# Down-projection in float32r: each product of 128 rows as two of 64 rows, with two accumulators

## The chip, the core and the metric

The kernel runs on one core of a Trainium2 chip. The time is the device time of one execution in microseconds; before the change it is 773.02 us in the median of three runs (772.6 to 773.74). A smaller time is better. A profiled execution gives the trace that this document reads. In it PE is TensorE's matmuls, PEld its weight loads, DVE is VectorE, ACT is ScalarE, POOL is GpSimd, SP is SyncE, whose queue issues most transfers.

## The reference

One layer of a causal decoder on 512 tokens of width 1024: an HGRN2 mixer and an S5 mixer side by side, a gated merge with an output projection, a conv-gated MLP, and a gated input embedding (PLE) with a last RMSNorm. The change lies in the last product of the MLP:

```python
def _conv_gated_ffn(h, w_up, conv_w, conv_b, w_down):
    a = h @ w_up                                   # (512, 1024) @ (1024, 5632)
    ...
    gate, val = jnp.split(c, 2, axis=-1)
    return (jax.nn.gelu(gate) * val) @ w_down      # (512, 2816) @ (2816, 1024)

x = x + _conv_gated_ffn(_rmsnorm(x, norm_ffn_g[i]), w_up[i], conv_w[i], conv_b[i], w_down[i])
ple_gate = jax.nn.sigmoid(_rmsnorm(x, norm_ple_g[i]) @ w_ple_gate[i])
x = x + ple_gate * (p[i] @ w_ple_proj[i])
return _rmsnorm(x, norm_final_g)
```

Everything is float32.

## The kernel before

Activations lie with their features on the 128 partitions and the 512 tokens along the free dimension. Every large product takes its operands in two float32r parts, a high one (a copy rounded to float32r) and a low one (what the rounding left), and adds three matmuls into one PSUM bank: high weights by high activations, high by low, low by high. `mm3` (L229) issues these three, at L231, L232 and L233, and then calls `tick`, which advances side work by an estimated clock.

Weights stream from HBM in pieces of at most 1024 columns (`emit_w`, L202 issues the transfer into `wst`, of which there are two). `split` (L243 on ScalarE, L244 on VectorE) makes `whi` and `wlo`, of which three pairs exist. For the last stage, the gates, the pairs are called `wgh` and `wgl` and all eight stay in place.

The MLP's up-projection (`pup`, `pug`, `puv`) leaves 22 row blocks of 128 features as pairs `gh`, `gl`. The down-projection runs four passes (`mp2`). In each, two blocks of 128 output features are summed over the 22 row blocks, one bank each (`pdn`): 22 x 2 x 3 = 132 products a pass, 528 in all. After a pass `finish_x` adds each sum to the residual `xr` (L945, VectorE), makes the split pair `x2gh` (L946, ScalarE) and `x2gl` (L947, VectorE), and squares `xr` (L953, ScalarE); GpSimd adds the squares up in `sqs` (L954). During the following pass a side generator transposes the two finished blocks on TensorE, four transposes a block (`ptk`, L1031), and ScalarE copies them out (L1033).

After the last pass come the PLE projection (`ppe`), with the transposes of the last two blocks between, the sums over `sqs` (`psq`), and the gates (`pga`, then `pgb`).

TensorE's order is the order in which the program is written. The other engines' orders are made by a scheduler, which puts `split` of weights at high priority; so instructions added on VectorE can move others. There are four large PSUM buffers (`main_ps`) and four for small uses (`small_ps`), a bank each; `pdn` takes large ones, `ptk` and `psq` small ones.

Of the kernel before, what the change touches and what calls it, by code (L numbers as in the profile page):

```python
# [12 lines left out]
ALU = mybir.AluOpType  # L13
# [3 lines left out]
P = 128  # L17
# [4 lines left out]
NJ = FF // P  # L22
# [91 lines left out]
def hybrid_kernel(ctx: ExitStack, tc: tile.TileContext, a):  # L114
    nc = tc.nc
    V, S, G, E = nc.vector, nc.scalar, nc.gpsimd, nc.tensor
# [13 lines left out]
    def main_ps(name):  # L130
        return psm.tile([P, 512], F32, tag="main", name=name)

    def small_ps(name):
        return pss.tile([P, 512], F32, tag="small", name=name)
# [8 lines left out]
    def small(name, j=0, w=1):  # L143
        return sm[:, OFF[name] + j: OFF[name] + j + w]
# [4 lines left out]
    clock = [0.0]  # L149
    sides = []  # L150

    def tick():
        for sd in list(sides):
            if sd[0] <= clock[0]:
                d = next(sd[1], None)
                if d is None:
                    sides.remove(sd)
                else:
                    sd[0] = clock[0] + d

    def side(gen, delay=0.0):
        sides.append([clock[0] + delay, gen])
        return sides[-1]
# [61 lines left out]
    def get_w():  # L225
        prefetch_w()
        return wstate["ready"].pop(0)

    def mm3(out, w, x, start, stop):  # L229
        (wh, wl), (xh, xl) = w, x  # L230
        E.matmul(out, wh, xh, start=start, stop=False)  # L231
        E.matmul(out, wh, xl, start=False, stop=False)  # L232
        E.matmul(out, wl, xh, start=False, stop=stop)  # L233
        clock[0] += 0.65
        tick()

    def cols(w, kk, width, c0, n=P):

        return tuple(t[:, kk * width + c0: kk * width + c0 + n] for t in w)
# [6 lines left out]
    def act_pair(name):  # L246
        return (ap_.tile([P, KD, T], F32R, tag="ahi", name=name + "h"),
                ap_.tile([P, KD, T], F32R, tag="alo", name=name + "l"))
# [140 lines left out]
    def k_outer(name, out4, x, then=None):  # L389

        ps = [main_ps(f"{name}{m}") for m in range(4)]
        k = 0
        while k < KD:
            nk = plan[wstate["next"] - len(wstate["ready"])][0][2]
            w = get_w()
            for kk in range(nk):
                for m in range(4):
                    mm3(ps[m], cols(w, kk, 512, m * P), rows(x, k), k == 0, k == KD - 1)
                k += 1
        if then:  # L400
            then()
        for m in range(4):
            out4(m, ps[m])
# [28 lines left out]
    def phase_v():  # L432
        ps = [main_ps(f"psv{t}") for t in range(4)]
        for k0 in range(0, KD, 2):
            w = get_w()
            for kk in range(2):
                k = k0 + kk
                for t in range(4):
                    mm3(ps[t], tuple(x[:, k, t * P:(t + 1) * P] for x in xg), cols(w, kk, 512, 0, 512),
                        k == 0, k == KD - 1)  # L440
        for t in range(4):
            S.activation(vt[t], ps[t], AF.Copy, scale=rr1[:, t:t + 1])
# [17 lines left out]
    def proj(name, pool=main_ps):  # L460
        w = get_w()
        ps = pool(name)
        for k in range(KD):
            mm3(ps, cols(w, k, P, 0), rows(xg, k), k == 0, k == KD - 1)
        return ps
# [453 lines left out]
    for m in range(KD):  # L919
        w = get_w()  # L920
        ps = [main_ps(f"pbh{m}"), main_ps(f"pbs{m}")]
# [3 lines left out]
        a_, b_ = (sig[m][:, i] for i in range(2))  # L925
# [9 lines left out]
    xr = xp.tile([P, KD, T], F32, name="xr")  # L935
# [6 lines left out]
    def finish_x(m, ps, x, g):  # L942

        xm = xr[:, m]
        V.tensor_tensor(out=xm, in0=xm, in1=ps, op=ALU.add)  # L945
        S.activation(x[0][:, m], xm, AF.Copy, scale=small(g, m))  # L946
        V.scalar_tensor_tensor(out=x[1][:, m], in0=xm, scalar=small(g, m), in1=x[0][:, m].bitcast(F32),  # L947
                               op0=ALU.mult, op1=ALU.subtract)
        if m == 0:
            S.activation(sqs, xm, AF.Square)  # L950
        else:
            sq = xp.tile([P, T], F32, tag="sq", bufs=2, name=f"sq{m}")
            S.activation(sq, xm, AF.Square)  # L953
            G.tensor_tensor(out=sqs, in0=sqs, in1=sq, op=ALU.add)  # L954
# [17 lines left out]
    for m in range(4, KD):  # L972
        w = get_w()
        ps = main_ps(f"pw{m}")
# [8 lines left out]
    gs_ = [(gpool.tile([P, T], F32R, name=f"gh{j}"), gpool.tile([P, T], F32R, name=f"gl{j}")) for j in range(NJ)]  # L983
# [19 lines left out]
    ps = [main_ps(f"pup{i}") for i in range(4)]  # L1003
    r2 = r2_sums()
    next(r2)
    for k0 in range(0, KD, 2):
        w = get_w()
# [7 lines left out]
    for j in range(2, NJ):  # L1015
        ps = [main_ps(f"pug{j}"), main_ps(f"puv{j}")]
        for k0 in (0, 4):
            w = get_w()
# [16 lines left out]
    def tok_side(ms):  # L1035
        for m in ms:
            to_tokens(m)
            yield 0.0

    x2 = act_pair("x2g")  # L1040
    for mp2 in range(KD // 2):
        ps = [main_ps(f"pdn{mp2}_{i}") for i in range(2)]
        for k0 in range(0, NJ, 4):
            w = get_w()
            for kk in range(min(4, NJ - k0)):
                k = k0 + kk
                for i in range(2):
                    mm3(ps[i], cols(w, kk, 256, i * P), gs_[k], k == 0, k == NJ - 1)
        for i in range(2):
            finish_x(mp2 * 2 + i, ps[i], x2, "g_ple")  # L1050
        if mp2 < 3:
            side(tok_side((mp2 * 2, mp2 * 2 + 1)), 8.0)

# [49 lines left out]
    ps = [[main_ps(f"pga{t}{c}") for c in range(2)] for t in range(2)]  # L1103
# [90 lines left out]
def build(arrays):  # L1194
    import concourse.bacc as bacc
    nc = bacc.Bacc("TRN2", target_bir_lowering=False, num_devices=1, dynamic_dma_scratch_size=8192)
    args = {n: nc.dram_tensor(n, v.shape, mybir.dt.from_np(v.dtype), kind="ExternalInput").ap()
            for n, v in arrays.items()}
    args["out"] = nc.dram_tensor("out", (4, P, D), F32, kind="ExternalOutput").ap()
    with tile.TileContext(nc) as tc:  # L1200
        hybrid_kernel(tc, args)
    return nc
# [9 lines left out]
```

## Time and profile before

| what | value |
| --- | --- |
| median of three runs | 773.02 us |
| the profiled execution | 772.75 us |
| its span, first to last instruction | 771.0 us |
| granted TensorE clock, mean over the span | 0.998 |
| PE busy | 759.0 us (98%) |
| DVE busy | 517.6 us (67%) |
| ACT busy | 367.5 us (48%) |
| POOL busy | 54.6 us (7%) |
| down-projection, first product to end of the last | 585.10 to 707.60 us |

A group of instructions reads: line, engine, operation, what is written and read (buffer numbers left out), shape, count, then busy time in us, mean ns of one, idle time before them. A matmul's shape `128*64 128x512` is rows times columns of the array, then what streams. A timeline row begins with start and duration in us. A row of a stretch gives its bounds and length, then for each engine that works there the busy time and the count, the granted clock, the DMA share and GB/s. Matmuls overlap, so a matmul's duration is not its price: the distance of starts is. After a change of what the engine does, a matmul's start is shown at the start of its load.

### The profile page before, as it was taken

To read this page: it belongs to the slowest core of one execution; us is meant where nothing else is said; L and a number is where in the kernel's file an instruction comes from. 1 tells how busy PE (TensorE), PEld (TensorE's weight loads), DVE (VectorE), ACT (ScalarE), POOL (GpSimd) and SP (SyncE) were. 2 spreads that over 40 slices of the span, in tenths; PEclk is the share of its full clock that TensorE was granted. 3 is DMA by queue.
4 is the path that set the end of the run, shared out by engine and by line. 5 is a ranking of instruction groups with operands and counts; after the bars stand their busy time and mean duration, and the time that the engine had idled before them with its cause. 6 is when DMAs were issued, how large, how long until landed. Compare 5 with 4: busy or idle time off the path is not lost.

```text
span 771.0 us, 10253 instructions
## 1 busy us (share of the span) xinstructions
PE 759.0 (98%) x3966; PEld 627.7 (81%) x3966; DVE 517.6 (67%) x851; ACT 367.5 (48%) x480; POOL 54.6 (7%) x96
## 2 busy tenths in 40 slices
PE   9999999999999999999999999999999999999996
PEld 7887888888887888888888888888888888888885
DVE  6999897798946675467976677677776324144555
ACT  7364583775748533342634344434434223234465
POOL 2030110010010000041000000000000001011000
PEclk9999999999999999999999999999999999999999
DMA  8573443243443323532232323232322332233511
GB/s 333 211 179 100 108 104 106 69 114 101 110 110 96 110 82 126 179 106 93 99 101 91 109 82 110 83 109 86 107 91 87 95 109 91 90 96 136 164 55 54
DMA packets 27039, 86.37 MB, mean 112 GB/s; under 512 B 4720, under 2 KB 4864, under 8 KB 26992
## 3 DMA queue, kind: packets, MB, share of 16 engines
q1 hardware_dynamic: 22608, 77.84, 30.7%
q0 software_dynamic: 3664, 6.84, 4.0%
q10 hardware_dynamic: 720, 1.05, 0.4%
q8 instruction: 31, 0.51, 0.3%
q14 instruction: 16, 0.13, 0.1%
HBM read 80.98 MB, written 4.69 MB: 111 GB/s over the span
## 4 chain that ended last, share of the span: by engine, by line
PE 90%; DVE 5%; DMA 2%; ACT 1%; issue 1%; POOL 0%; DVEq 0%; ACTq 0%
PE pdn L233 5%; PE pdn L231 5%; PE pdn L232 5%; PE puv L231 5%; PE puv L233 5%; PE pug L231 5%; PE pug L232 5%; PE pug L233 5%; PE puv L232 5%; PE pw L231 2%; PE pw L232 2%; PE pw L233 2%; PE pgs L231 2%; PE pgh L231 2%; PE pgs L233 2%; PE pgs L232 2%
## 5 line engine op out<-in xcount | busy, mean ns | idle before, releaser
L243 ACT ACTIVATE whi<-wst 128x1024 fp32r<-128x1024 f32 (+1 forms) x124 | 128.8, 1038 | 253.5 <-issue 75.1
L244 DVE TENSOR_TENSOR wlo<-wst,whi 128x1024 fp32r<-128x1024 f32 (+1 forms) x124 | 148.4, 1197 | 115.1 <-ACT whi L243 115.0
L231 PE MATMUL pdn<-gh,whi 128*128 128x512 f32 x176 | 69.1, 393 | 0.0
L233 PE MATMUL pdn<-gh,wlo 128*128 128x512 f32 x176 | 68.6, 390 | 0.0
L232 PE MATMUL pdn<-gl,whi 128*128 128x512 f32 x176 | 68.6, 390 | 0.0
L232 PE MATMUL pug<-x1gl,whi 128*128 128x512 f32 x160 | 62.3, 390 | 0.0
L233 PE MATMUL puv<-x1gh,wlo 128*128 128x512 f32 x160 | 62.3, 390 | 0.0
L231 PE MATMUL puv<-x1gh,whi 128*128 128x512 f32 x160 | 62.3, 390 | 0.0
L231 PE MATMUL pug<-x1gh,whi 128*128 128x512 f32 x160 | 62.3, 389 | 0.0
L232 PE MATMUL puv<-x1gl,whi 128*128 128x512 f32 x160 | 62.3, 389 | 0.0
L233 PE MATMUL pug<-x1gh,wlo 128*128 128x512 f32 x160 | 62.3, 389 | 0.0
L992 DVE TENSOR_TENSOR u<-pug,R 128x512 f32<-128x512 f32 x20 | 13.8, 692 | 38.4 <-PE pug L233 38.4
L954 POOL TENSOR_TENSOR sqs<-sqs,sq 128x512 f32<-128x512 f32 x14 | 23.2, 1658 | 229.1 <-ACT sq L953 225.0
L233 PEld LDWEIGHTS pdn<-gh,wlo 128*128 128x128 f32 x176 | 33.0, 188 | 6.9
L232 PEld LDWEIGHTS pdn<-gl,whi 128*128 128x128 f32 x176 | 33.1, 188 | 6.7
L231 PEld LDWEIGHTS pdn<-gh,whi 128*128 128x128 f32 x176 | 33.1, 188 | 6.6
L233 PEld LDWEIGHTS puv<-x1gh,wlo 128*128 128x128 f32 x160 | 30.1, 188 | 6.3
L232 PEld LDWEIGHTS pug<-x1gl,whi 128*128 128x128 f32 x160 | 30.1, 188 | 6.2
L233 PEld LDWEIGHTS pug<-x1gh,wlo 128*128 128x128 f32 x160 | 30.0, 188 | 6.3
L232 PEld LDWEIGHTS puv<-x1gl,whi 128*128 128x128 f32 x160 | 30.0, 188 | 6.2
L231 PEld LDWEIGHTS puv<-x1gh,whi 128*128 128x128 f32 x160 | 30.1, 188 | 6.1
L231 PEld LDWEIGHTS pug<-x1gh,whi 128*128 128x128 f32 x160 | 30.0, 188 | 6.2
(391 smaller groups left out, 1751.6 us busy)
## 6 DMA issues: line engine op xcount, KB each, us to landing
wst<-W SPq DMA_DIRECT2D x126, 512.0 KB, 3.3
xt<-x SPq DMA_DIRECT2D x4, 512.0 KB, 9.2
T<-d_k POOLq DMA_DIRECT2D x4, 512.0 KB, 8.6
xr<-xT SPq DMA_DIRECT2D x4, 512.0 KB, 6.4
wst<-W SPq DMA_DIRECT2D x6, 256.0 KB, 2.5
xs<-xT SPq DMA_DIRECT2D x4, 256.0 KB, 5.4
xs<-xT SPq DMA_DIRECT2D x2, 512.0 KB, 6.4
d_u<-uT POOLq DMA_DIRECT2D x4, 256.0 KB, 5.0
```

The lines of the kernel that those rows point to most:

```text
L231: E.matmul(out, wh, xh, start=start, stop=False)
L232: E.matmul(out, wh, xl, start=False, stop=False)
L233: E.matmul(out, wl, xh, start=False, stop=stop)
L243: S.activation(hi, src, AF.Copy)
L244: return V.tensor_tensor(out=lo, in0=src, in1=hi.bitcast(F32), op=ALU.subtract)
L954: G.tensor_tensor(out=sqs, in0=sqs, in1=sq, op=ALU.add)
L992: V.tensor_tensor(out=u[:, 2:], in0=ps[i], in1=Rt, op=ALU.mult)
```

## The change

Each product of the down-projection is issued as two, with the same moving columns and weight columns: one on partitions 0 to 63, one on partitions 64 to 127. The first adds into `pdn`, a large buffer, the second into a new accumulator `pdm`, a small one. After a pass VectorE adds `pdm` to the residual (a new instruction, L1061 of the changed program) before `finish_x` adds `pdn`. Ten lines come in ahead, so L231 is still `mm3`'s, and what was L244, L945, L947 and L1031 stands at L254, L955, L957 and L1041.

```diff
+    def mm3_rows(outs, w, x, start, stop):
+
+        (wh, wl), (xh, xl) = w, x
+        for i, (a_, b_) in enumerate(((wh, xh), (wh, xl), (wl, xh))):
+            for r, o in enumerate(outs):
+                rr = slice(r * 64, (r + 1) * 64)
+                E.matmul(o, a_[rr], b_[rr], start=start and i == 0, stop=stop and i == 2)
+        clock[0] += 0.65
+        tick()
...
     for mp2 in range(KD // 2):
-        ps = [main_ps(f"pdn{mp2}_{i}") for i in range(2)]
+        ps = [(main_ps(f"pdn{mp2}_{i}"), small_ps(f"pdm{mp2}_{i}")) for i in range(2)]
...
-                    mm3(ps[i], cols(w, kk, 256, i * P), gs_[k], k == 0, k == NJ - 1)
+                    mm3_rows(ps[i], cols(w, kk, 256, i * P), gs_[k], k == 0, k == NJ - 1)
         for i in range(2):
-            finish_x(mp2 * 2 + i, ps[i], x2, "g_ple")
+            m = mp2 * 2 + i
+            V.tensor_tensor(out=xr[:, m], in0=xr[:, m], in1=ps[i][1], op=ALU.add)
+            finish_x(m, ps[i][0], x2, "g_ple")
```

On TensorE, the first row block of the first pass before (the two output blocks are `pdn_0` and `pdn_1`):

```order
L231 MATMUL pdn_0_4989<-gh_3153,whi_4906 128x512
L232 MATMUL pdn_0_4989<-gl_3154,whi_4906 128x512
L233 MATMUL pdn_0_4989<-gh_3153,wlo_4907 128x512
L231 MATMUL pdn_1_4990<-gh_3153,whi_4906 128x512
L232 MATMUL pdn_1_4990<-gl_3154,whi_4906 128x512
L233 MATMUL pdn_1_4990<-gh_3153,wlo_4907 128x512
```

and in the changed program:

```order
L243 MATMUL pdn_0_4989<-gh_3153,whi_4906 128x512
L243 MATMUL pdm_0_4990<-gh_3153,whi_4906 128x512
L243 MATMUL pdn_0_4989<-gl_3154,whi_4906 128x512
L243 MATMUL pdm_0_4990<-gl_3154,whi_4906 128x512
L243 MATMUL pdn_0_4989<-gh_3153,wlo_4907 128x512
L243 MATMUL pdm_0_4990<-gh_3153,wlo_4907 128x512
L243 MATMUL pdn_1_4991<-gh_3153,whi_4906 128x512
L243 MATMUL pdm_1_4992<-gh_3153,whi_4906 128x512
```

The halves of a product follow each other, and every second instruction goes to the other half and bank: 1056 instead of 528. The transposes stand between the same products as before.

On VectorE, the end of the fourth pass before (`wlo` is the split of the last piece for `ppe`, `wgl` those of the first gate pieces):

```order
L945 TENSOR_TENSOR xr<-xr,pdn_0_5557 128x512
L945 TENSOR_TENSOR xr<-xr,pdn_1_5558 128x512
L244 TENSOR_TENSOR wlo_5754<-wst_5751,whi_5753 128x1024
L947 SCALAR_TENSOR_TENSOR x2gl<-xr,sm,x2gh 128x512 x2
L244 TENSOR_TENSOR wgl_5765<-wst_5780,wgh_5764 128x1024
```

and in the changed program:

```order
L1061 TENSOR_TENSOR xr<-xr,pdm_0_5966 128x512
L955 TENSOR_TENSOR xr<-xr,pdn_0_5965 128x512
L1061 TENSOR_TENSOR xr<-xr,pdm_1_5968 128x512
L254 TENSOR_TENSOR wlo_6298<-wst_6295,whi_6297 128x1024
L254 TENSOR_TENSOR wgl_6309<-wst_6324,wgh_6308 128x1024
L957 SCALAR_TENSOR_TENSOR x2gl<-xr,sm,x2gh 128x512
L955 TENSOR_TENSOR xr<-xr,pdn_1_5967 128x512
L957 SCALAR_TENSOR_TENSOR x2gl<-xr,sm,x2gh 128x512
```

The last addition to the residual has moved behind two weight splits and one `x2gl`. On ScalarE, after the same pass, the changed program has

```order
L253 ACTIVATE whi_6297<-wst_6295 128x1024
L253 ACTIVATE wgh_6308<-wst_6324 128x1024
L956 ACTIVATE x2gh<-xr,sm 128x512
L963 ACTIVATE sq_6285<-xr 128x512
L1085 ACTIVATE pe<-ppe_6356 128x512
L1085 ACTIVATE pe<-ppe_6364 128x512
L1085 ACTIVATE pe<-ppe_6372 128x512
L956 ACTIVATE x2gh<-xr,sm 128x512
L963 ACTIVATE sq_6292<-xr 128x512
```

where before both pairs of `x2gh` and square stood ahead of the gate's `wgh` and of the copies `pe`. The last square, which `psq` on TensorE waits for by way of GpSimd, is now last of these nine.

## The prediction

> **What bounds the kernel now.** First the page: busy time, then the chain of work that ended last, then the down-projection's group.
>
> ```profile
> span 771.0 us, 10253 instructions
> ...
> PE 759.0 (98%) x3966; PEld 627.7 (81%) x3966; DVE 517.6 (67%) x851; ACT 367.5 (48%) x480; POOL 54.6 (7%) x96
> ...
> PE 90%; DVE 5%; DMA 2%; ACT 1%; issue 1%; POOL 0%; DVEq 0%; ACTq 0%
> ...
> L231 PE MATMUL pdn<-gh,whi 128*128 128x512 f32 x176 | 69.1, 393 | 0.0
> ```
>
> TensorE carries the chain and never idles before these products. The third view is the busy time of the stretch from the first product of the down-projection to the end of the last: all work, then the tile `pdn` alone, then the transposes `ptk` alone.
>
> ```profile
> 585.10:707.60 122.50, 122.50 (x554) 101.50 (x553) 42.55 (x45) 36.74 (x47) 8.21 (x5) 1.00 0.29 91
> ...
> 585.10:707.60 122.50, 121.35 (x528) 98.51 (x527) 4.59 (x7) 1.00 0.29 91
> ...
> 585.10:707.60 122.50, 3.60 (x24) 2.99 (x24) 3.58 (x6) 1.00 0.29 91
> ```
>
> 528 products and 24 transposes fill 122.50 us without a gap (PE busy 122.50); VectorE is busy for a third of it (42.55), ScalarE for less. So the price of one product decides. Not its 393 ns, which overlap, but the distance between starts. The timeline, matmuls and then weight loads:
>
> ```profile
> 599.83 0.39 PE L233 MATMUL pdn<-gh,wlo 128*128 128x512 f32 x1
> ...
> 602.10 0.39 PE L231 MATMUL pdn<-gh,whi 128*128 128x512 f32 x1
> ...
> 599.83 0.19 PEld L231 LDWEIGHTS pdn<-gh,whi 128*128 128x128 f32 x1
> 600.06 0.19 PEld L232 LDWEIGHTS pdn<-gl,whi 128*128 128x128 f32 x1
> ```
>
> From 599.83 to 602.10 lie ten products: **0.227 us each**, and 528 x 0.227 = 119.9 us. Each load starts when the product before starts and is over (0.19) before that product has streamed: loading is hidden already. What the change is worth is therefore 528 times what a pair of halves costs above or below 0.227, and whatever surrounds the pairs.
>
> The Trainium skill, page "TensorE: Matmul & The Clock Gate", section "Part 3: Packing small matmuls", says that a weight load overlaps running matmuls only where the row groups differ; by that rule loads of full height lie open today and the split would hide them, a gain. The rows of 599.83 disagree: the load runs inside the product before it, on the same rows.
>
> **The pair of halves.** Every product becomes two, on rows 0 to 63 and 64 to 127, each with all 128 weight columns and all 512 moving columns. If halves run in turn, a pair costs 2 x 0.227 = 0.454. If they run side by side, it costs what one does, provided that two loads fit. How fast loads can follow one another, and what a shorter product costs:
>
> ```profile
> 125.27 0.64 PEld L172 LDWEIGHTS pu<-vt,b 128*128 128x128 f32 x5
> ...
> 762.52 0.28 PE L231 MATMUL ppe<-whi,whi 128*128 128x256 f32 x1
> ...
> 763.59 0.28 PE L231 MATMUL ppe<-whi,whi 128*128 128x256 f32 x1
> ```
>
> Five loads in 0.64, the last of them 0.19 long: (0.64 - 0.19) / 4 = 0.113 from load to load. Two loads one after the other take 0.226, just inside 0.227; overlapped, they take less. Nine products of 256 columns lie between 762.52 and 763.59: 0.119 each, so the second 256 columns of a full product cost 0.108 and 512 would cost 0.216 without the fixed part of 0.011. Lower bound of a pair: 0.216, if that fixed part vanished behind the other half (528 x 0.011 = 5.8 us gained). Upper bound: 0.454 (528 x 0.227 = 119.9 us lost).
>
> Which end? The trace holds no product on half the rows, but products on half and quarter columns of the array; the chain gives their pace, the groups their shapes.
>
> ```profile
> 125.42 0.67 PE pu L172 x6
> 126.09 1.08 PE ps5v L172 x32
> ...
> 153.47 0.57 PE ps5k L758 x16
> ...
> L172 PE MATMUL ps5v<-uy,et 128*64 128x64 f32 x128 | 4.6, 225 | 0.0
> ...
> L172 PE MATMUL pu<-vt,b 128*128 128x128 f32 x24 | 3.3, 274 | 0.0
> L758 PE MATMUL ps5k<-F,Bb 128*32 128x128 f32 x64 | 2.6, 279 | 0.0
> ```
>
> A full-array pass of 128 moving columns takes 0.67 / 6 = 0.112. The passes of `ps5k` move 128 columns too, on four column strips in turn: 0.57 / 16 = 0.036, a third. Half-width `ps5v` passes of 64 columns cost 0.034 where half of 0.112 is 0.056. Products on different parts of the array do run together here, their loads too. Row halves differ in one thing: column strips write different partitions of PSUM, row halves write the same 128 partitions of two banks at once. No row shows that; I take the value of the strips, **0.227 a pair, 0 us**, and keep both ends.
>
> The same section of the Trainium skill puts about 4 ns of issue time on each further tile of a pack. By it, an estimate, the stage would lose 528 x 0.004 = 2.1 us more; no row here shows row tiles.
>
> **Changing the mode.** Going between full-array and partial products costs. Into `ps5y` (half columns) and out of it, loads and matmul:
>
> ```profile
> 139.93 0.19 PEld L233 LDWEIGHTS pgs<-xgh,wlo 128*128 128x128 f32 x1
> 140.47 0.20 PEld L172 LDWEIGHTS ps5y<-st,F 128*64 128x64 f32 x4 [0.35 <-issue]
> ...
> 140.15 0.39 PE L233 MATMUL pgs<-xgh,wlo 128*128 128x512 f32 x1
> ...
> 142.21 0.20 PEld L172 LDWEIGHTS ps5y<-uy,T 128*64 128x64 f32 x4
> 142.48 0.19 PEld L231 LDWEIGHTS pgh<-xgh,whi 128*128 128x128 f32 x1
> 142.59 0.19 PEld L232 LDWEIGHTS pgh<-xgl,whi 128*128 128x128 f32 x1
> ```
>
> The last full product starts at 140.15 and has streamed at 140.38; the first load of the new mode waits until 140.47 instead of following at 140.16. So 0.09 of emptying, and the load is no longer hidden: 0.11 for 128 columns. 0.20 per change. On the way out the last of four loads starts near 142.27, its product is through near 142.38, and the next full product streams when the second load follows, 142.59: 0.21. In the down-projection the transposes are full-array:
>
> ```profile
> 623.63 0.59 PEld L1031 LDWEIGHTS ptk<-sm,xr 128*128 128x128 f32 x4
> 624.19 0.19 PEld L231 LDWEIGHTS pdn<-gh,whi 128*128 128x128 f32 x1
> 624.30 0.19 PEld L232 LDWEIGHTS pdn<-gl,whi 128*128 128x128 f32 x1
> ```
>
> Today their first load starts with the last product before them, at no cost. There are 24 / 4 = 6 groups, each with a change in and one out, and the stage's own entry and exit: 14 changes x 0.205 = **+2.9 us**. Nothing hides them, since TensorE is the chain.
>
> **The second sums and the order behind them.** Eight more additions on VectorE of about 0.69 (half of the 1.37 below): 5.5 us on an engine that is busy for a third of the stage; off the path. From the third pass on the new accumulators take the banks of the transposes of the pass before, which run some 8 us into a pass of 122.5 / 4 = 30.6 us; ScalarE has emptied them long before the next pass starts, and no product waits for a bank. At the end of the stage the order changes, and TensorE soon needs the sum of squares:
>
> ```profile
> 707.12 1.37 DVE L945 TENSOR_TENSOR xr<-xr,pdn 128x512 f32<-128x512 f32 x2
> ...
> 707.57 1.06 ACT L243 ACTIVATE whi<-wst 128x1024 fp32r<-128x1024 f32 x1 [1.66 <-PE pdn L232]
> ...
> 710.28 0.61 ACT L953 ACTIVATE sq<-xr 128x512 f32<-128x512 f32 x1
> 710.80 1.05 ACT L243 ACTIVATE wgh<-wst 128x1024 fp32r<-128x1024 f32 x1
> ...
> 709.90 3.50 POOL L954 TENSOR_TENSOR sqs<-sqs,sq 128x512 f32<-128x512 f32 x2 [27.39 <-ACT sq L953]
> ...
> 716.46 1.08 PEld L172 LDWEIGHTS psq<-ones,sqs 128*128 128x128 f32 x8
> ...
> L244 DVE TENSOR_TENSOR wgl<-wst,wgh 128x1024 fp32r<-128x1024 f32 x8 | 10.9, 1362 | 7.1 <-ACT wgh L243 7.1
> L947 DVE SCALAR_TENSOR_TENSOR x2gl<-xr,sm,x2gh 128x512 fp32r<-128x512 f32 x8 | 8.7, 1134 | 0.0
> ```
>
> `psq` is issued at 716.46; the sums were ready at 709.90 + 3.50 = 713.40, 3.1 us early. Now the last addition stands behind `wgh`, `wgl` and one `x2gl`. If the gate weights land by 710.80, the latest that this row allows: wgh to 711.85, wgl to 713.2, x2gl to 714.35, addition to 715.0, x2gh (0.7) and square (0.61) to 716.3, POOL (1.75) to 718.1: TensorE waits 1.4. If they land by 708.63, when `whi` ends: wgl follows the other split (from 709.2, 1.23) at 710.4 and all is some 1.5 earlier: no wait. I take **+0.7**. Queued behind `psq` are only gate products, which come later by as much.
>
> **Sum.** The profiled execution took 772.75 us, 0.27 below the median of 773.02: 772.75 + 0 + 2.9 + 0.7 = 776.35. I say **776.5 us**; this case alone holds 774.8 to 779 (four ns a pair, 0 to 1.4 at the end, the changes at half to one and a half).
>
> **Rivals.**
> *The halves run in turn*, because both write the same partitions, or because the program's half is run like a full product. For it: no row shows two writers of one partition. Against: strips share everything else and overlap. 772.75 + 119.9 + 3.6 = 896.
> *A load must be finished before the other half's may begin*: 2 x 0.188 = 0.376 a pair, + 78.7 + 3.6 = 855. Against it: loads follow at 0.113.
> *Some contention*, a few to 40 ns a pair (loads fit by only 0.001): 0.240 would give 772.75 + 6.9 + 3.6 = 783, 0.260 gives 794.
> *Faster*: one half's fixed 0.011 passes behind the other's stream, since two products now stand at the array. It decides once it saves over 3.6 / 528 = 0.007 a pair; all of it gives 772.75 - 5.8 + 3.6 = 770.6. Against it: each half keeps its own row of load, product, load; only what the two share could shrink, and the rows do not say that the 0.011 is shared.
>
> **How the numbers follow.** Forecast 0.60, in turn 0.11, serial loads 0.03, contention 0.12, faster 0.14. About 0.2% (1.5 us) is what a measurement can tell here. Faster than that: most of the last case, 0.10. Same: the rest of it and the low edge of the forecast, 0.13. Slower: 0.77. For 8 in 10 the range leaves out 896 and 855 (0.14), the worst contention (0.03) and the best gain (0.03): 770 to 792.
>
> **What would show it.** In the new profile the two halves' rows start a few ns apart and pairs 0.227 apart; `pdn` and `pdm` together have 1056 matmuls in about 125.4 us; before each `ptk` group and after it the loads pause by 0.2; `psq` starts up to 1.4 late. Pairs 0.45 apart, or halves of 0.227 in turn, would refute the core of it; pairs under 0.220 would make the change a gain.

## The result

| | median, us | lowest to highest |
| --- | --- | --- |
| the kernel before (9 executions) | 773.02 | 772.22 to 775.46 |
| the changed kernel (9 executions) | 778.16 | 775.55 to 779.42 |

The ratio is 1.0063, with a 95% interval of 1.0047 to 1.0078: slower by 0.6%. The profiled execution of the changed kernel took 778.16 us; the one of before took 772.75.

### The profile page after: what moved, and what is told of

Same layout as the page of the kernel before. It is cut to its first block, busy times and chain, and to the rows that moved or that the text cites. A ratio compares the mean times of both kernels' runs of the same rounds, so it can differ in the third digit from the quotient of the medians.

```text
span 776.4 us, 11316 instructions
## 1 busy us (share of the span) xinstructions
PE 762.3 (98%) x4494; PEld 626.8 (81%) x4494; DVE 521.7 (67%) x859; ACT 368.0 (47%) x480; POOL 53.0 (7%) x96
## 4 chain that ended last, share of the span: by engine, by line
PE 85%; DVE 6%; DMA 5%; ACT 2%; issue 1%; SPq 0%; POOL 0%; ACTq 0%; DVEq 0%
PE pdm L243 9%; PE pdn L243 6%; PE pug L233 5%; PE puv L233 5%; PE puv L231 5%; PE pug L231 5%; PE puv L232 5%; PE pug L232 5%; PE pw L233 2%; PE pw L232 2%; PE pw L231 2%; PE pgh L231 2%; PE pgs L231 2%; PE pgs L233 2%; PE pgs L232 2%; PE pgh L232 2%
## 5 line engine op out<-in xcount | busy, mean ns | idle before, releaser
L254 DVE TENSOR_TENSOR wlo<-wst,whi 128x1024 fp32r<-128x1024 f32 (+1 forms) x124 | 149.0, 1202 | 111.1 <-ACT whi L253 111.0
L243 PE MATMUL pdn<-gh,whi 64*128 64x512 f32 x176 | 68.8, 391 | 0.0
L243 PE MATMUL pdm<-gh,whi 64*128 64x512 f32 x176 | 68.7, 390 | 0.0
L243 PE MATMUL pdm<-gh,wlo 64*128 64x512 f32 x176 | 68.0, 386 | 0.0
L243 PE MATMUL pdn<-gh,wlo 64*128 64x512 f32 x176 | 68.0, 386 | 0.0
L243 PE MATMUL pdm<-gl,whi 64*128 64x512 f32 x176 | 68.0, 386 | 0.0
L243 PE MATMUL pdn<-gl,whi 64*128 64x512 f32 x176 | 68.0, 386 | 0.0
L231 PE MATMUL pug<-x1gh,whi 128*128 128x512 f32 x160 | 62.2, 389 | 0.0
L231 PE MATMUL puv<-x1gh,whi 128*128 128x512 f32 x160 | 62.2, 389 | 0.0
L243 PEld LDWEIGHTS pdm<-gh,wlo 64*128 64x128 f32 x176 | 32.4, 184 | 4.5
L243 PEld LDWEIGHTS pdm<-gl,whi 64*128 64x128 f32 x176 | 32.4, 184 | 4.2
L243 PEld LDWEIGHTS pdm<-gh,whi 64*128 64x128 f32 x176 | 32.4, 184 | 4.2
L243 PEld LDWEIGHTS pdn<-gh,whi 64*128 64x128 f32 x176 | 32.4, 184 | 3.9 <-issue 1.4
```

The source lines that it names most:

```text
L243: E.matmul(o, a_[rr], b_[rr], start=start and i == 0, stop=stop and i == 2)
L254: return V.tensor_tensor(out=lo, in0=src, in1=hi.bitcast(F32), op=ALU.subtract)
```

## The profile after

The page first, as for before: span, busy time, the chain that ended last, and two groups of the down-projection.

```profile
span 776.4 us, 11316 instructions
...
PE 762.3 (98%) x4494; PEld 626.8 (81%) x4494; DVE 521.7 (67%) x859; ACT 368.0 (47%) x480; POOL 53.0 (7%) x96
...
PE 85%; DVE 6%; DMA 5%; ACT 2%; issue 1%; SPq 0%; POOL 0%; ACTq 0%; DVEq 0%
...
L243 PE MATMUL pdn<-gh,whi 64*128 64x512 f32 x176 | 68.8, 391 | 0.0
L243 PE MATMUL pdm<-gh,whi 64*128 64x512 f32 x176 | 68.7, 390 | 0.0
```

TensorE is still the chain. There are 528 matmuls more, and each group of halves has the duration that the full products had (390 ns). The stretch of the down-projection, from its first product to the first `ppe`: all work, then `pdn`, `pdm` and `ptk` alone.

```profile
587.15:711.92 124.77, 124.77 (x1082) 100.87 (x1081) 46.84 (x51) 37.00 (x47) 6.85 (x5) 1.00 0.28 89
...
587.15:711.92 124.77, 121.66 (x528) 96.64 (x528) 4.09 (x6) 1.00 0.28 89
...
587.15:711.92 124.77, 121.65 (x528) 96.64 (x528) 4.67 (x7) 1.00 0.28 89
...
587.15:711.92 124.77, 3.93 (x24) 2.51 (x24) 3.58 (x6) 1.00 0.28 89
```

124.77 us where there were 122.50: **+2.27**. `pdn` and `pdm` are each busy for nearly the whole stretch, at the same time. The timeline inside a pass, matmuls and then weight loads:

```profile
600.00 0.39 PE L243 MATMUL pdn<-gh,wlo 64*128 64x512 f32 x1
600.00 0.39 PE L243 MATMUL pdm<-gh,wlo 64*128 64x512 f32 x1
...
601.36 0.39 PE L243 MATMUL pdn<-gh,wlo 64*128 64x512 f32 x1
601.36 0.39 PE L243 MATMUL pdm<-gh,wlo 64*128 64x512 f32 x1
...
600.00 0.18 PEld L243 LDWEIGHTS pdn<-gh,whi 64*128 64x128 f32 x1
600.00 0.18 PEld L243 LDWEIGHTS pdm<-gh,whi 64*128 64x128 f32 x1
```

Six pairs lie between 600.00 and 601.36: 1.36 / 6 = 0.227 a pair, as one full product took. Both halves start within some 3 ns, and so do their loads, each 0.18 long where a load of 128 rows took 0.19. The halves run side by side, and the pair neither gains nor loses.

What the stage lost lies at the transposes. One group before and one after:

```profile
623.63 0.39 PE L233 MATMUL pdn<-gh,wlo 128*128 128x512 f32 x1
623.86 0.60 PE L1031 MATMUL ptk<-sm,xr 128*128 128x128 f32 x4
624.22 0.48 PE L231 MATMUL pdn<-gh,whi 128*128 128x512 f32 x1
624.53 0.40 PE L232 MATMUL pdn<-gl,whi 128*128 128x512 f32 x1
```

```profile
625.84 0.39 PE L243 MATMUL pdn<-gh,wlo 64*128 64x512 f32 x1
...
626.16 0.66 PE L1041 MATMUL ptk<-sm,xr 128*128 128x128 f32 x4
626.74 0.49 PE L243 MATMUL pdn<-gh,whi 64*128 64x512 f32 x1
...
627.08 0.39 PE L243 MATMUL pdn<-gl,whi 64*128 64x512 f32 x1
```

From the last product ahead of the group to the second behind it: 624.53 - 623.63 = 0.90 before, 627.08 - 625.84 = 1.24 after, 0.34 for two changes of mode. The kernel before pays almost nothing here: transposes follow each other every 0.108 in its trace, and 2 x 0.227 + 4 x 0.108 = 0.89, so 0.01 is left (the product at 624.22 is shown at the start of its load).

The changed kernel's trace also shows where the 0.34 lies. On the way in, the load of the second transpose starts at 626.21, so the first one streams from there; without a change it would have streamed from 625.84 + 0.227 = 626.06. That is 0.15, of which 0.06 is the open load (626.15 to 626.21). On the way out, the fourth transpose starts at 626.54 and has streamed at 626.65; the first pair streams when the second pair's load starts, at 626.85. That is 0.20.

The rest is behind the stage. The waits of TensorE, after, have two lines that the list of before lacks:

```profile
PE pf L233 <- DVE wlo L254: 0.7, 1, 0.7
PE ppe L231 <- ACT pe L1085: 0.6, 1, 0.6
```

The second is in the PLE projection. Timeline after, ScalarE, VectorE and GpSimd, then TensorE:

```profile
714.65 1.06 ACT L253 ACTIVATE wgh<-wst 128x1024 fp32r<-128x1024 f32 x1 [1.79 <-DMA wst<-W]
...
716.75 1.55 ACT L1085 ACTIVATE pe<-ppe 128x512 f32<-128x512 f32 x3
...
717.55 0.68 DVE L955 TENSOR_TENSOR xr<-xr,pdn 128x512 f32<-128x512 f32 x1
...
719.66 1.28 POOL L964 TENSOR_TENSOR sqs<-sqs,sq 128x512 f32<-128x512 f32 x1 [0.87 <-ACT sq L963]
...
716.13 0.60 PE L1041 MATMUL ptk<-sm,xr 128*128 128x128 f32 x4
717.38 0.50 PE L231 MATMUL ppe<-whi,whi 128*128 128x512 f32 x1 [0.65 <-ACT pe L1085]
...
722.10 0.95 PE L172 MATMUL psq<-ones,sqs 128*128 128x2 f32 x8
```

The squares are not what TensorE waits for: the last sum is ready at 719.66 + 1.28 = 720.94, 1.2 ahead of `psq`. It waits for a bank. There are four large ones. The first two `ppe` take the two that the last pass leaves free, the third takes that of the first `pdn`. The last addition of a `pdn` ends at 717.55 + 0.68 = 718.23, since it stands behind the split of gate weights for which ScalarE waits 1.79; so the fourth `ppe` has the bank of the first `ppe`, and that is free when the first copy `pe` is out (716.75 + 0.57). From the transposes to this `ppe` it takes 717.38 - 716.13 = 1.25 where it took 0.35. From the first `ppe` to `psq` it is 722.10 - 711.92 = 10.18, before 9.10: **+1.08**.

2.27 + 1.08 = 3.35, and 0.1 more at the entry, where the first pair comes 0.32 instead of 0.227 behind the last product of the up-projection: 3.45. The two profiled executions differ by 5.41. The remaining 2.0 lies ahead of the down-projection, where the programs are the same: its first product starts at 587.15, before at 585.10. The stretch in which most of that arises, after and then before (the value ahead of the last two is the granted clock):

```profile
220.00:250.00 30.00, 28.15 (x128) 23.22 (x128) 12.05 (x17) 22.28 (x25) 3.04 (x4) 0.94 0.35 106
```

```profile
220.00:250.00 30.00, 28.29 (x136) 23.58 (x135) 14.02 (x20) 24.02 (x27) 3.05 (x4) 1.00 0.39 106
```

A clock of 0.94 over 30 us costs 0.06 x 30 = 1.8 us. Closer by, it is one spell of half clock, behind a wait of TensorE:

```profile
237.99 0.49 PE L172 MATMUL pso<-q,St 128*128 128x128 f32 x2 [1.85 <-DVE St L571]
...
239.37 0.63 PE L231 MATMUL pgh<-xgh,whi 128*128 128x512 f32 x1
239.79 0.63 PE L232 MATMUL pgh<-xgl,whi 128*128 128x512 f32 x1
```

From 239.00 to 242.00 the granted clock is 0.50 and products come every 0.43 us. The whole spell lasts 3.4 us and costs half of that, 1.7 us. A repetition of the changed kernel has 1.00 at this place, but a spell of the same length near 73 us. Of the eleven profiles of this case, eight have such a spell of 3.4 us at half clock ahead of the down-projection, near 74 or near 240 us, and one of the eight is of the kernel before, with its transposes spread (below). In these eight the down-projection starts at 585.43 to 587.26 us, in the three without a spell at 584.80 to 585.10.

So the remaining 2.0 is that spell and some tenths. The mean granted clock tells how many spells an execution has: the profiles without one have 0.998 or 0.999, those with one 0.995 to 0.997, the one with two 0.993 (1.7 us of 771 are 0.002). The fairest comparison is therefore at equal clock (executions of the two programs in the comparisons below and, of the changed kernel, above; a few at other values are left out):

| granted clock | before: executions, mean us | changed: executions, mean us | difference |
| --- | --- | --- | --- |
| 0.998 | 7, 772.73 | 1, 775.55 | 2.8 |
| 0.997 | 5, 774.24 | 2, 778.10 | 3.9 |
| 0.996 | 24, 773.99 | 6, 777.55 | 3.6 |
| 0.994 | 2, 776.53 | 1, 779.52 | 3.0 |
| 0.993 | 2, 775.39 | 4, 779.06 | 3.7 |

Weighted by the executions of the changed kernel that is 3.5, as the rows have it (3.45). The rest of the difference of the medians (778.16 - 773.02 = 5.1) goes with the clock, which was low more often in the changed kernel's executions: 0.994 or less in 6 of 15, in the kernel before in 4 of 43.

## The experiments

**The kernel before and the changed kernel once more**, to see how large a difference is that means nothing, and whether the first comparison holds. No edit.

> The kernel before once more, to learn its scatter and its granted clock. In the changed kernel's runs the clock lies between 0.992 and 0.998 and the time rises with it going down, from 775.55 to 779.42 us. If such clock spells come to any version by chance, this kernel shows them too: single executions of 772 to 776 us, with the longer ones at the lower clock. If the half products lower the clock, all of these runs stand at 0.998 and within 1 us of 773.0.

The kernel before against itself: ratio 0.9998, 0.9986 to 1.0009; its own executions lie between 772.46 and 775.63. First product of the down-projection at 584.80, before at 585.10. So 0.2% can be told, and a shift of some tenths ahead of the stage says nothing. The clock lies between 0.993 and 0.998 here too, and the longest execution is the one at 0.993: the spells come without half products, as was expected of chance.

> The changed kernel once more, beside the one before. My theory (14 changes of mode at 0.17 us and a late square sum of 1.1 us, pairs at the price of one product): 773.0 + 2.3 + 1.1 = 776.4 at a clock of 0.998, more only by clock spells. The rival (the changed kernel costs 5 us by itself, whatever the clock): 778 at 0.998 too. In the trace both expect the first pdn to first ppe in 124.8 us against 122.5.

Ratio 1.0054, 1.0037 to 1.0071, median 777.93. The stage took 124.77 again to the hundredth, `ppe` to `psq` 10.14. The two terms repeat; the start of the stage (585.91 here, 587.15 there) does not. No execution had a clock of 0.998 this time; the one that had, in the first comparison, took 775.55, which fits the 776.4 better than the rival's 778.

**The late order at the end.** The additions and what follows from them at high priority, so that the gate's splits no longer go ahead of them:

```diff
         for i in range(2):
             m = mp2 * 2 + i
-            V.tensor_tensor(out=xr[:, m], in0=xr[:, m], in1=ps[i][1], op=ALU.add)
-            finish_x(m, ps[i][0], x2, "g_ple")
+            with tc.high_priority():
+                V.tensor_tensor(out=xr[:, m], in0=xr[:, m], in1=ps[i][1], op=ALU.add)
+                finish_x(m, ps[i][0], x2, "g_ple")
```

> The changed kernel with the additions and finish_x at high priority, so that the last square no longer stands behind a gate split. My theory: first ppe to psq falls from 10.2 us back to 9.1, the time falls by 1.1 us against the changed kernel; the stage before stays 124.8. The rival, that the late sum costs nothing because TensorE makes it up before the gates: no change of the time.

776.22 us, ratio 1.0031 (1.0019 to 1.0043), 1.7 us below the repetition of the changed kernel; at a clock of 0.993, the only one of the table's values that both have, 777.89 (3 executions) against 779.06 (4), 1.2 below, where 1.1 was expected. The stage is unchanged (124.77), `ppe` to `psq` falls from 10.18 to 9.22: 0.96 of the 1.08. TensorE's wait for `pe` is gone from its list of waits. The timeline shows why, VectorE, TensorE, ScalarE:

```profile
712.70 0.68 DVE L955 TENSOR_TENSOR xr<-xr,pdn 128x512 f32<-128x512 f32 x1
...
714.77 0.48 PE L231 MATMUL ppe<-whi,whi 128*128 128x512 f32 x1
...
715.06 0.58 ACT L1086 ACTIVATE pe<-ppe 128x512 f32<-128x512 f32 x1
```

The first copy `pe` comes no earlier than in the changed kernel (5.44 us behind the first `ppe` against 5.41), but the fourth `ppe` starts ahead of it, at 714.77: it no longer needs that bank, since the last addition has freed its own at 713.38. So the late addition is the cause of 0.96, by way of the bank. The remaining 0.1 fits the part of the change of mode that lies behind the first `ppe`: a change out costs 0.20, and 0.09 of it is ahead of that `ppe`.

**No transposes within the down-projection.** All six blocks are transposed in a row behind it, so that the stage has one mode:

```diff
-        if mp2 < 3:
-            side(tok_side((mp2 * 2, mp2 * 2 + 1)), 8.0)
...
+    for m in range(6):
+        to_tokens(m)
```

> The changed kernel with the six transposed blocks moved from inside the passes to the end of the down-projection, in a row: 12 of the 14 changes of mode are gone. My theory: the stage (first pdn to first ppe) falls from 124.8 to 122.7 us, 528 x 0.2267 + 24 x 0.11 + 2 x 0.17, unless ScalarE's copies hold the row of transposes up; the time falls by 2.1 us. The rival, that pairs themselves are slower than full products by 0.004 us each: the stage stays at 124.8.

From the first to the last `pdn` 119.61 us, where the changed kernel has 124.45: 4.84 less, of which 24 x 0.11 = 2.64 are the transposes themselves and 2.20 the twelve changes, 0.18 each. But the time is 779.9 (ratio 1.0074, 1.0056 to 1.0093). The list of waits, and then ScalarE's timeline, say where the gain went:

```profile
PE ptk L1041 <- ACT x2tok L1043: 3.3, 1, 3.3
...
709.63 1.06 ACT L253 ACTIVATE wgh<-wst 128x1024 fp32r<-128x1024 f32 x1 [1.76 <-DMA wst<-W]
...
711.73 1.54 ACT L1043 ACTIVATE x2tok<-ptk 128x512 f32<-128x512 f32 x3
```

There are four small banks, so the fifth block of transposes waits until ScalarE has copied one out, and the copies stand behind the same `wgh` that waits for its weights. The gain of 2.2 was given back to a wait of 3.3. Behind this wait stands a second spell at half clock: from 712.40 to 715.90 the granted clock is 0.51, which costs another 1.7 us in the profiled execution. Five of the six executions have a mean clock of 0.993 or less.

**The price of a change of mode by itself.** The same 24 transposes, one at a time instead of four together: 24 groups instead of 6, so 36 changes more. The same edit was made in the kernel before, where no mode changes, to take away what the spreading itself costs.

```diff
-            to_tokens(m)
-            yield 0.0
+            ps = small_ps(f"ptk{m}")
+            for t in range(4):
+                E.transpose(ps[:, t * P:(t + 1) * P], xr[:, m, t * P:(t + 1) * P], ident)
+                clock[0] += 0.11
+                yield 0.0
+            S.activation(x2tok[:, :, m * P:(m + 1) * P], ps.rearrange("p (t c) -> p t c", t=4), AF.Copy)
```

> The changed kernel with one transpose at a time between products instead of four: 24 groups, 48 changes of mode inside the stage instead of 12. By the changes measured in the changed kernel (0.17 us each): 36 x 0.17 = 6.3 us more, stage 131.0 us. By the price of the prediction (0.205): 7.4 more, 132.2. If changes of mode cost nothing and the loss lies elsewhere: 124.8.

> The same splitting of the transposes in the kernel before, where everything is full-array: no change of mode, the stage stays at 122.5 us within 0.5. If single transposes cost by themselves (a load that finds no product to hide behind), the stage grows here too, and that share is to be taken off the run with half products.

The stretches, in the changed kernel and in the kernel before:

```profile
586.76:718.01 131.25, 131.25 (x1082) 100.31 (x1081) 46.84 (x51) 36.65 (x47) 6.85 (x5) 1.00 0.27 85
```

```profile
585.78:708.48 122.70, 122.70 (x554) 100.68 (x552) 42.54 (x45) 36.40 (x47) 8.20 (x5) 1.00 0.28 90
```

131.25 - 124.77 = 6.48, less 122.70 - 122.50 = 0.20, over 36: **0.174 us a change**, as the first expectation had it (131.0). Fourteen of them are 2.44; the stage with its entry and exit shows 2.27 + 0.1 + 0.1. The mean of 0.15 on the way in and 0.20 on the way out is the same. Both runs are of one execution each (784.26 and 773.65 us).

**Both halves on the same rows.** Both products use rows 0 to 63, so rows 64 to 127 are left out and the result is not the kernel's; instructions, banks and modes are otherwise those of the changed kernel.

```diff
             for r, o in enumerate(outs):
-                rr = slice(r * 64, (r + 1) * 64)
+                rr = slice(0, 64)
```

> The changed kernel with both products of a pair on rows 0 to 63 (rows 64 to 127 of every block are left out, the upper rows counted twice). Same instructions, banks and counts. If it is the different rows that let the halves overlap, they now run in turn: 1056 x 0.227 = 239.7, the stage 244.7 us, about 898 us in all, the price of my rival 'in turn'. If any two products into different banks overlap, the stage stays at 124.8 us.

```profile
586.24:830.72 244.48, 244.48 (x1081) 196.31 (x1080) 45.24 (x52) 37.39 (x47) 7.47 (x5) 1.00 0.16 49
...
599.99 0.39 PE L243 MATMUL pdn<-gh,whi 64*128 64x512 f32 x1
...
600.22 0.39 PE L243 MATMUL pdm<-gh,whi 64*128 64x512 f32 x1
```

896.04 us (one execution), the stage 244.48: what the rival of halves in turn would have given. A half product has the pace of a full one (0.227), so a pair at 0.227 in the changed kernel is a whole overlap, and different rows are its condition. The end tells something too: the stage lasts longer, the gate's weights have landed, `wgh` follows `whi` at once (831.34 behind 830.38), the copy `pe` is out 3.28 us behind the first `ppe` instead of 5.41, and though the order is the changed kernel's, `ppe` to `psq` takes 9.22. In these two runs the same order costs time where the weights come late, and none where they are there.

**Three halves on one side, then three on the other.** The order within a product is turned, so that the same rows come three times in a row:

```diff
-        for i, (a_, b_) in enumerate(((wh, xh), (wh, xl), (wl, xh))):
-            for r, o in enumerate(outs):
+        for r, o in enumerate(outs):
+            for i, (a_, b_) in enumerate(((wh, xh), (wh, xl), (wl, xh))):
```

> The changed kernel with the loops exchanged: first the three products of the upper half, then the three of the lower. If TensorE starts products strictly in order, only the third of one half and the first of the other run side by side: six half products take four steps of 0.227 us instead of three, 704 x 0.227 + 2.6 + 2.4 = 164.8 us for the stage, 40 more, about 818 us in all. If each half works through its own queue, the stage stays near 124.8 us.

```profile
587.26:712.07 124.81, 124.81 (x1081) 102.17 (x1080) 46.49 (x51) 36.78 (x46) 6.83 (x5) 1.00 0.29 89
...
587.26 0.49 PE L243 MATMUL pdn<-gh,whi 64*128 64x512 f32 x1
587.27 0.49 PE L243 MATMUL pdm<-gh,whi 64*128 64x512 f32 x1
587.60 0.39 PE L243 MATMUL pdn<-gl,whi 64*128 64x512 f32 x1
```

The expectation failed: 124.81, not 164.8. In the program the first `pdm` is fourth, behind all three `pdn`; on the chip it starts some 10 ns after the first `pdn` and ahead of the other two. So halves on different rows do not start in the program's order. In the changed kernel too, the trace has the second half some 3 ns ahead of the first in 330 of the 528 pairs. The one execution took 778.71 us; from `ppe` to `psq` it has 10.56, as the wait for `pe` is 1.0 us here.

**As many instructions, no halves.** Each product as two of 256 tokens on all 128 rows, in two banks that are added as in the changed kernel: the program has the changed kernel's length (11316 instructions), and no change of mode. Each of the two additions to the residual takes the 256 columns of its bank.

```diff
-                rr = slice(r * 64, (r + 1) * 64)
-                E.matmul(o, a_[rr], b_[rr], start=start and i == 0, stop=stop and i == 2)
+                cc = slice(r * 256, (r + 1) * 256)
+                E.matmul(o[:, cc], a_, b_[:, cc], start=start and i == 0, stop=stop and i == 2)
...
```

> A program with as many instructions as the changed kernel, but each product of the down-projection is split by tokens, two products of 256 columns on all 128 rows, in two banks that are added as in the changed kernel; no product uses a part of the rows, so there is no change of mode. Stage from the first product of the down-projection to the first output block: about 528 x 2 x 0.119 + 2.64 = 128.3 us, if a product of 256 columns takes 0.119. Theory A (the length of the program delays its start: the wait of TensorE for wlo at 28 us that all kernels with split products show, and none of the others): the same wait of 0.4 to 0.9 us is there, and the first product of the down-projection starts at 585.4 us or later. Theory B (the halves of the rows have to do with it, or it is chance): no such wait, first product at 584.8 to 585.5 us. Total about 779 to 781 us.

781.98 us, 1 above what was expected, ratio 1.0099 (1.0083 to 1.0116). The stretch, and the line of TensorE's waits that is in question:

```profile
584.89:714.20 129.31, 129.31 (x1081) 129.31 (x1080) 43.18 (x52) 36.71 (x47) 8.23 (x5) 1.00 0.27 86
...
PE pf L233 <- DVE wlo L254: 0.7, 1, 0.7
```

129.31 rather than 128.3: products of 256 columns come every 0.120, and 1056 x 0.120 + 2.64 = 129.4. The wait at 28 us is here too. It stands in all eight profiles of programs of 11315 or 11316 instructions and in none of the three of 10253, so it goes with the length of the program (or something that comes with it), not with the halves, against theory B. But theory A had a second part, and this fell: the first product of the down-projection starts at 584.89, as early as in the kernel before. The 0.7 is made up on the way; it does not explain the lost time. The spells do: this profile has none, and the down-projection starts late only in the eight profiles that have one. Why the changed kernel, by its mean clock, had two of them more often stays open.

## Why the prediction was right

Predicted 776.5 us, slower by 3.6 than the profiled execution; measured 778.16 in the median, 5.1 above the median before, and 3.5 slower at equal clock (3.45 by the rows). The mechanism was right in its two main terms. That the sum comes so near is partly luck: one term was 0.4 too high and the other 0.3 too low, and the second came about by another way than the one described.

- *The pair of halves at 0.227, 0 us.* Right: 0.227 in the timeline, and the overlap is that of different rows (244.48 us on the same rows). It was taken over from column strips, which no row then showed for row halves; it held. Neither bound came: the fixed 0.011 is not hidden behind the other half, so the faster rival fell; loads of both halves run together, so the rivals of serial loads and of contention fell. The rule of the Trainium skill ("TensorE: Matmul & The Clock Gate", "Part 3: Packing small matmuls") that loads overlap only where row groups differ promised a gain that did not come: 0.227 before and after. The 4 ns that the Trainium skill gives there for a further tile are seen as the 3 ns between the two starts, but they fall inside the pair and do not add up to the 2.1 us.
- *Fourteen changes of mode, 2.9 us.* The mechanism and the count were right, the price was too high: 0.174 each, 2.44 in all. The term that was mis-sized is the way into the transposes, priced at 0.20: the emptying of 0.09 came as predicted, but the load of the first transpose stands open for 0.06 and not for the 0.11 that was read off `ps5y`, so the way in costs 0.15, six times. The way out, priced at 0.21, measured 0.20. About 0.01 a group was paid in the kernel before.
- *0.7 at the end, between 0 and 1.4.* The size came out at 0.98 (1.08 less the 0.1 of the mode), inside the bounds, and the cause was right, the last addition behind the gate's splits, together with the time at which the weights land: with the additions at high priority 0.96 is gone, and with the weights there early there is no wait. The way from cause to wait was wrong: TensorE did not wait for the sum of squares, so that the bounds held is luck. The step that failed is "no product waits for a bank", which was looked up for the next pass of the down-projection and not for the `ppe` behind the last.
- *What the sum left out.* That the two programs are equal ahead of the down-projection was taken to mean that this part takes equally long. In medians it did not, by 1.7 us in the first comparison and 0.7 in the repetition, and the table of clocks accounts for it; the cause of the spells was not found.
- *The range of this case.* 774.8 to 779 does not follow from the terms named beside it: with all of them at their ends they give 772.75 + 1.45 = 774.2 and 772.75 + 2.1 + 4.35 + 1.4 = 780.6.
- *Queue order.* That three halves of one side ahead of three of the other would cost a third more was expected only of that experiment; it fell.

## What to carry to other kernels

A product of 512 columns split by rows costs what it cost whole (0.227 us), so long as the halves are on different rows; on the same rows each half costs as much as the whole. So splitting a product that fills the rows buys nothing. Count instead what the split puts around the products: each change between halves and the full array costs 0.17 us on TensorE in the mean, and an additional sum can move an order on another engine. When an instruction moves back on its engine, follow the buffers that it frees as well as what reads its result.

## What was not expected of the hardware

- Halves on different rows do not start in program order: with three of one side issued ahead of three of the other, both sides still started within 3 to 13 ns of each other, 0.227 apart (stage 124.81 us, 164.8 expected).
- A short pause of TensorE can be followed by 3.4 us at half clock. In the changed kernel's profile it waits 1.85 us at 236 us, and from 239 to 242 us its products are 0.43 apart instead of 0.227; in the profile of before it waits 1.7 us at the same place, and the clock stays at 1.00. In the repetition of the changed kernel a wait of 2.2 us near 72 us is followed by such a spell, in the repetition of the kernel before one of 2.8 us at that place is not. The Trainium skill ("TensorE: Matmul & The Clock Gate", "Part 1: The HAM clock gate") tells of a window of 3.4 us that runs freely; the length of the spells agrees with it. The Trainium skill has the clock fall there after about one idle window of 3.4 us; here shorter pauses were enough, in some executions and not in others. No run here varies the pause.
- The longer programs have a wait of TensorE of 0.4 to 0.9 us at 28 us that the shorter ones, equal up to there, have not (eight profiles against three); in one of the longer programs it was made up before the down-projection. Its cause is not known.
